# The first expert layer's input and the query weights begin one word into longer rooms

## The chip, the cores and the metric

The kernel runs on one core of a Trainium2 chip. A core has five engines that run side by side, each with its own instruction stream: TensorE (PE, matrix products; its weight loads are shown as PEld), VectorE (DVE), ScalarE (ACT), GpSimd (POOL) and SyncE (SP, which only issues transfers here). They share an on-chip memory of 128 partitions; PE writes its results into a second memory, PSUM, from which ACT and DVE take them. The metric is the device time of one execution in microseconds (us). The kernel before takes 1811.01 us (median of 3 runs, 1810.87 to 1811.89).

## The reference: what is computed

One layer of a decoder, for 512 tokens of width 1024 and 256 memory tokens, all in float32. The hidden state is normalized and projected, three mixers run on it (causal pooling, a sparse attention with 16 heads, a cross-attention into the memory), their outputs are gated, merged and added. The second half is the part that the change touches:

```python
def block(xb):                       # xb: 128 normalized tokens
    q = (xb @ w_q).reshape(n, PEER_HEADS, 2, PEER_HALF)
    s = jnp.einsum('nhpc,hpkc->nhpk', q, sub_keys)
    s_top, i_top = lax.top_k(s, PEER_TOPK)
    ...
    ids = jnp.take_along_axis(cand_i, best_pos, axis=-1)
    gate = jax.nn.softmax(best_s, axis=-1)
    act = jax.nn.gelu(jnp.einsum('nd,nhkd->nhk', xb, u[ids]), approximate=False)
    return jnp.einsum('nhk,nhkd->nd', gate * act, v[ids])
```

It is a layer of 128 x 128 = 16,384 experts of one neuron each. A token picks 16 experts for each of 8 heads by the sums of two sub-key scores; `u` is the experts' first layer, `v` the second. A last normalization gives the output.

## The kernel before

**Products of three parts.** TensorE's fast float32 type (float32r) keeps fewer bits. So each operand is split into a high part (the rounded value, an ACT copy, L133) and a low part (the rest, a subtraction on DVE or POOL, L134), and a product is high x high + high x low + low x high. `mm3_steps` (L154, L161) issues it: for eight contraction steps of 128, three matmuls each, 24 in all, that add up in one PSUM tile. The weights are the stationary side (128 x 128, loaded anew for each matmul); the token side moves, 512 columns for all tokens.

**The feed.** `feed` holds the list of all weight tiles in the order of use. `fetch` issues a tile's load on SP (L78), `part` splits it into `wh` and `wl`, `take` hands it to the matmuls and runs the two ahead by one or two tiles. Most tiles live in one pool with two rooms per part. The list can name another pool for a tile, with three rooms per part: `opool` for three of the four weight pieces of the output projection's second half, and `qpool` for the query weights from the third on (14 of 16).

**The input of the first layer.** `hfh` and `hfl` are the high and low part of the normalized tokens, transposed: 128 partitions, eight contraction steps of 512 words. `transpose_split` writes them, per token block in two halves: a transpose on PE (L192), the high part by ACT (L195), the low part by DVE (L196).

**Who reads them.** `q_mm`, 16 query tiles, all 512 columns. `hidden`, 128 tiles of the first layer, 352 columns, since the first token block and the 32 tokens after it go another way (their experts' rows are gathered one by one). The first tile of either kind takes `mm3_steps`' other order (L154); all others are L161.

**The order of the work from the output projection on.** The output projection (L1166: here the tokens' parts are stationary and the weights move) ends in the normalization and the transposes. Then come the 16 query tiles, each followed by eight matmuls for its scores (L1250) while DVE picks the best (MAX8 and others). Then `lead`: 70 first-layer tiles, whose results wait in HBM, beside the selection on DVE and the gate matrices on PE (one-hot matmuls of 128 columns in float16, L1475, evacuated by ACT at L1478). Last `experts`: 56 first-layer tiles, each beside the second layer of the tile before (18 matmuls of 512 columns, L1634), then 72 second-layer tiles alone. POOL gathers single rows for the first token block all the while. The order on each engine is written out by hand.

**Where things lie.** Pools are stacks from the left and the right end of the memory, tiles follow each other in the order of their allocation, and a tile of four bytes takes 32. Small tiles named `pad` stand in many pools. The `wh`, `wl`, `hfh`, `hfl`, `hnh`, `hnl`, `wgh` and `wgl` tiles all begin at a multiple of 64 bytes, and so does every one of their rows that a matmul reads. `hfh`, `hfl` and behind them the pool `n2` (the tokens, the normalization's rows, and the `opool` rooms) lie on the left; when `n2` is closed, `wv2` with the second layer's weights takes its place, beginning with the tile `seen`. Of `seen` one column is written, to make POOL wait for a load. The query weights' rooms, the sub-keys `skt` and the scores lie in a pool on the right.

Of the kernel before, what the change touches and what calls it, by code (L numbers as in the profile page):

```python
# [10 lines left out]
F32 = mybir.dt.float32  # L11
F32R = mybir.dt.float32r
# [9 lines left out]
T = 512  # L22
NB = 4
D = 1024
KD = 8
# [30 lines left out]
        yield from x  # L56


class Feed:


# [20 lines left out]
    def part(self, n):  # L82
        while self.np < min(n, len(self.specs)):
            key, src, nk, m, eng, other = self.specs[self.np]
            pool, bufs = (self.pool, 2) if other is None else (other[0], 3)
            hi = pool.tile([128, nk, m], F32R, tag=self.tag + "h", name="wh", bufs=bufs)
            lo = pool.tile([128, nk, m], F32R, tag=self.tag + "l", name="wl", bufs=bufs)
            self.split(hi, lo, self.raw.pop(self.np)[0].rearrange("p (k n) -> p k n", n=m), eng or self.nc.gpsimd)
            self.w[self.np] = (hi, lo)
            self.np += 1  # L90
# [20 lines left out]
def layer(ctx: ExitStack, tc: tile.TileContext, A: dict, out: bass.AP, dbg=None):  # L111
# [8 lines left out]
    def sbuf(stack, name, side="left"):  # L120
        return stack.enter_context(tc.tile_pool(name=name, bufs=1, side=side, reuse_waits="tile"))

    def psum(tag, shape, bufs=2, dt=F32):
        return ps.tile(shape, dt, tag=tag, name=tag, bufs=bufs)
# [469 lines left out]
    for c in cross_order:  # L594
        n = int(c[1]) if c[1:].isdigit() else None
# [442 lines left out]
    for at in attention():  # L1038
# [5 lines left out]
        while done < goal:  # L1044
            c = next(filler, None)
# [55 lines left out]
    hrow = dram.tile([X, D], F32, name="hrow")  # L1101
    idd = dram.tile([X, 128], I32, name="idd")
    hp_ = sbuf(ctx, "hp")
    hfh = hp_.tile([128, KD, T], F32R, name="hfh")
    hfl = hp_.tile([128, KD, T], F32R, name="hfl")
    n2s = ExitStack()
    n2 = sbuf(n2s, "n2")
    opool.append(n2)
# [47 lines left out]
    for half, tags in ((0, "SSoo"), (1, "zzSS")):  # L1156
# [12 lines left out]
        if half == 0:  # L1169

            for k2 in range(4):
                w = feed.take(("o", 0, k2))
# [120 lines left out]
    for hp in range(16):  # L1293
        if hp < 15:
            p = psum("z", [128, T])
# [273 lines left out]
    def vfetch(m, eng=nc.sync):  # L1569
        if m < 128:  # L1570
            j = order[m]
            VR[m] = wv2.tile([128, 1024], F32, tag="wr", name="wr", bufs=5)
            eng.dma_start(VR[m], A["v_rows"][j * 128:(j + 1) * 128])
# [155 lines left out]
    gath = seq(*[gathered(b) for b in range(GB)])  # L1729
    ost2.close()  # L1730
    wv2 = sbuf(hst, "wv2")
    seen = wv2.tile([128, 224], F32, name="seen")
    vfetch(0)
    vfetch(1)
    gload(0)
# [109 lines left out]
```

## Time and profile before

| what | value |
| --- | --- |
| median of 3 runs | 1811.01 us |
| the profiled execution: its own time | 1810.61 us |
| the profiled execution: span from first to last instruction | 1808.8 us |
| mean granted TensorE clock | 0.999 |
| PE busy, matmuls | 1787.7 us, 10098 |
| DVE, ACT, POOL busy | 1360.5, 837.7, 770.6 us |

The span is the time between the first and the last instruction that the profiler recorded; the execution's own time has the start and the end around it. Busy times are unions of an engine's instructions; matmuls overlap in the array, so their durations are longer than their distances. A group's row has the line, the engine and operation, the tile written and the tiles read, the shape, the count, the busy time and the mean duration in ns, and then the idle time before it. The chain is followed back from the last instruction, at each step to what released it.

### The profile page before, as it was taken

The numbers are of one execution on the slowest core, as the hardware profiler recorded it, in microseconds if no ns is written. First come the engines' busy times: TensorE is split into PE (matmuls) and PEld (weight loads), VectorE is DVE, ScalarE is ACT, GpSimd is POOL, SyncE is SP. The second block draws the span as 40 slices with busy tenths as digits, with TensorE's granted clock in tenths as the row PEclk, the third lists the DMA queues.
The fourth block names the chain that finished last, engine by engine and source line by source line (L and its number), as shares of the span: only waits on it lengthen the run. The fifth ranks groups of instructions, "written<-read, shape, count | busy, mean of one in ns | idle before, by whom it ended". The sixth has DMA issues, their size and how long they took to land.

```text
span 1808.8 us, 27962 instructions
## 1 busy us (share of the span) xinstructions
PE 1787.7 (99%) x10098; PEld 1586.5 (88%) x10098; DVE 1360.5 (75%) x2814; ACT 837.7 (46%) x1476; POOL 770.6 (43%) x595
## 2 busy tenths in 40 slices
PE   8999999999999999999999999999999999999998
PEld 7988888888888888999999998999999998888886
DVE  5453147766544369999898859998898999888886
ACT  6434257777642333464555543333334333333334
POOL 3333555555643333511222026666656664333320
PEclk9999999999999999999999999999999999999999
DMA  6225632112223432376999899999999999999992
GB/s 225 90 84 168 223 108 59 48 59 71 65 76 111 168 132 91 114 240 215 344 356 326 297 380 410 409 375 392 373 361 368 377 369 376 384 382 382 378 372 105
DMA packets 157147, 445.94 MB, mean 247 GB/s; under 512 B 15969, under 2 KB 61697, under 8 KB 154322
## 3 DMA queue, kind: packets, MB, share of 16 engines
q1 hardware_dynamic: 88050, 262.78, 40.4%
q0 software_dynamic: 41840, 152.10, 22.3%
q10 hardware_dynamic: 27120, 29.30, 4.9%
q8 instruction: 79, 1.29, 0.3%
q14 instruction: 58, 0.48, 0.1%
HBM read 402.11 MB, written 47.24 MB: 248 GB/s over the span
## 4 chain that ended last, share of the span: by engine, by line
PE 92%; DVE 3%; ACT 3%; POOL 1%; issue 1%; DMA 0%; DVEq 0%; SPq 0%; ACTq 0%; POOLq 0%
PE z L161 49%; PE S L1634 10%; PE tr L1634 10%; PE o L1634 9%; PE S L905 1%; PE tr L937 1%; PE S L1166 1%; PE o L953 1%; PE o L424 1%; ACT pr L918 1%; PE o L1475 1%; PE tr L1475 1%; PE S L1475 1%; PE o L1250 1%; DVE pr L915 1%
## 5 line engine op out<-in xcount | busy, mean ns | idle before, releaser
L133 ACT ACTIVATE wh<-wr 128x1024 fp32r<-128x1024 f32 (+2 forms) x365 | 372.3, 1025 | 164.4 <-PE z L161 45.1
L134 POOL TENSOR_TENSOR wl<-wr,wh 128x1024 fp32r<-128x1024 f32 (+2 forms) x110 | 242.8, 2208 | 318.0 <-ACT wh L133 269.7
L161 PE MATMUL z<-hfh,wh 128*128 128x352 f32 (+1 forms) x1136 | 375.5, 332 | 0.0
L161 PE MATMUL z<-hfl,wh 128*128 128x352 f32 (+1 forms) x1136 | 373.4, 330 | 0.0
L134 DVE TENSOR_TENSOR wl<-wr,wh 128x1024 fp32r<-128x1024 f32 x255 | 305.8, 1216 | 80.7 <-ACT wh L133 79.8
L1498 POOL DMA_INDIRECT ug<-in_v_rows_dram,ids x128 | 176.1, 1375 | 199.3 <-DVE x1g L1518 179.9
L1498 POOL DMA_INDIRECT ug<-in_u_rows_dram,ids x128 | 193.7, 1514 | 104.6 <-DVE ug L1512 85.2
L161 PEld LDWEIGHTS z<-hfl,wh 128*128 128x128 f32 x1136 | 214.1, 188 | 6.3
L161 PEld LDWEIGHTS z<-hfh,wh 128*128 128x128 f32 x1136 | 213.5, 188 | 6.9 <-ACT wh L133 0.5
L161 PE MATMUL z<-hfh,wl 128*128 128x352 f32 (+1 forms) x1136 | 213.3, 330 | 0.1
L161 PEld LDWEIGHTS z<-hfh,wl 128*128 128x128 f32 x1136 | 189.2, 188 | 5.1 <-POOL wl L134 0.4
L1215 ACT ACTIVATE hg<-z 128x352 f32<-128x352 f32 x128 | 59.5, 465 | 279.2 <-PE z L161 277.3
L133 ACT ACTIVATE wgh<-gh 128x384 fp32r<-128x384 f32 x128 | 67.4, 526 | 232.1 <-DVE gh L1613 230.3
L1518 DVE SCALAR_TENSOR_TENSOR x1g<-ug,wgt,x1g 128x1024 f32<-128x1024 f32 x128 | 163.9, 1280 | 1.1
L1512 DVE SCALAR_TENSOR_TENSOR ug<-ug,hf 128x1024 f32<-128x1024 f32 x128 | 152.3, 1217 | 5.9 <-DMA ug<-in_u_rows_dram,ids 5.9
L161 PE MATMUL z<-hnh,wh 128*128 128x512 f32 x384 | 150.7, 393 | 0.0
L161 PE MATMUL z<-hnl,wh 128*128 128x512 f32 x384 | 150.3, 391 | 0.0
L1401 POOL DMA_INDIRECT ux<-in_u_rows_dram,idx x32 | 52.1, 1629 | 171.8 <-DVE ux L1409 169.1
L926 POOL TENSOR_SCALAR pr<-pr,sm,gsig 128x128 f32<-128x128 f32 (+3 forms) x128 | 78.1, 613 | 77.9 <-DVE sm L1000 49.0
L134 DVE TENSOR_TENSOR wgl<-gh,wgh 128x384 fp32r<-128x384 f32 x128 | 71.8, 561 | 37.2 <-ACT wgh L133 37.2
L941 DVE TENSOR_TENSOR PB<-tr,PB 128x128 fp32r<-128x128 f32 (+3 forms) x128 | 62.5, 488 | 49.2 <-ACT PB L940 48.5
L161 PE MATMUL z<-hnh,wl 128*128 128x512 f32 x384 | 99.2, 393 | 0.0
(410 smaller groups left out, 3590.3 us busy)
## 6 DMA issues: line engine op xcount, KB each, us to landing
wr<-in_u_t_dram SPq DMA_DIRECT2D x128, 512.0 KB, 6.6
wr<-in_v_rows_dram SPq DMA_DIRECT2D x128, 512.0 KB, 9.0
wr<-in_w_z_dram SPq DMA_DIRECT2D x48, 512.0 KB, 3.6
gd<-stg ACTq DMA_DIRECT2D x11, 2048.0 KB, 15.4
hg<-hd SPq DMA_DIRECT2D x72, 176.0 KB, 9.2
gj<-gd SPq DMA_DIRECT2D x8, 1408.0 KB, 11.9
go<-gd SPq DMA_DIRECT2D x8, 1408.0 KB, 12.9
hd<-hg SPq DMA_DIRECT2D x60, 176.0 KB, 5.6
```

The costliest lines, as they stand in the source:

```text
L133: s.activation(hi, src, AF.Copy)
L134: (eng or v).tensor_tensor(lo, src, f(hi), op=OP.subtract)
L161: pe.matmul(p, w[a][:, k], xs(x[b], k), start=k == 0 and a == 0 and b == 0, stop=k == nk - 1 and a == 1)
L926: g.tensor_scalar(pr[:, 0:n], pr[:, 0:n], sm, gsig[:, qb, c:c + 1], op0=OP.mult, op1=OP.mult)
L941: return lambda: v.tensor_tensor(lo, pt[:, 0:qb + 1], f(hi), op=OP.subtract)
L1215: s.activation(hg[:, X:], p[:, X:NT], AF.Gelu)
L1401: g.indirect_dma_start(out=XR[k], out_offset=None, in_=A["u_rows"], in_offset=bass.IndirectOffsetOnAxis(ap=idx[:, k:k + 1], axis=0))
L1475: pe.matmul(pg[:, n], oa[:, t_ // 2, :, t_ % 2], ob[:, r, t_ // 2, :, t_ % 2], start=n == 0 and r == 0, stop=n == 3 and r == 1, skip_group ...
L1498: g.indirect_dma_start(out=row, out_offset=None, in_=src, in_offset=bass.IndirectOffsetOnAxis(ap=ids[:, b, k:k + 1], axis=0))
L1512: v.scalar_tensor_tensor(row, row, 1.0, hf[:, b], op0=OP.mult, op1=OP.mult, accum_out=act[:, m:m + 1])
L1518: v.scalar_tensor_tensor(X1[b], rows.pop(m), wgt[:, m - 128:m - 127], X1[b], op0=OP.mult, op1=OP.add)
L1634: pe.matmul(acc_o[2 * b + half], a[:, b * 128:(b + 1) * 128], c[:, half], start=k == 0 and i == 0, stop=k == 127 and i == 2)
```

## The change

A helper `behind` makes a tile that is 64 words longer than the data, and returns the view that begins at word AT = 1 of it. `hfh` and `hfl` are made by it, and so are the `wh` and `wl` rooms of the feed's tiles that live in another pool (`opool` and `qpool`). Everything that writes or reads them uses the shifted view. `seen` becomes 128 words (512 bytes) shorter, as much as the rooms of `hfh` and `hfl` become longer together, so that the tiles behind it keep their places.

```diff
+AT = 1
+
+
+def behind(pool, name, k, n, **kw):
+
+    t = pool.tile([128, k * n + 64], F32R, name=name, **kw)
+    return t[:, AT:AT + k * n].rearrange("p (k n) -> p k n", n=n)
+
 class Feed:
...
             pool, bufs = (self.pool, 2) if other is None else (other[0], 3)
-            hi = pool.tile([128, nk, m], F32R, tag=self.tag + "h", name="wh", bufs=bufs)
-            lo = pool.tile([128, nk, m], F32R, tag=self.tag + "l", name="wl", bufs=bufs)
+            if other is None:
+                hi, lo = (pool.tile([128, nk, m], F32R, tag=self.tag + c, name="w" + c, bufs=bufs) for c in "hl")
+            else:
+                hi, lo = (behind(pool, f"w{c}", nk, m, tag=self.tag + c, bufs=bufs) for c in "hl")
...
-    hfh = hp_.tile([128, KD, T], F32R, name="hfh")
-    hfl = hp_.tile([128, KD, T], F32R, name="hfl")
+    hfh, hfl = behind(hp_, "hfh", KD, T), behind(hp_, "hfl", KD, T)
...
-    seen = wv2.tile([128, 224], F32, name="seen")
+    seen = wv2.tile([128, 96], F32, name="seen")
```

## The prediction

> **What bounds the kernel now.** I read the page first, then the groups of instructions by shape, the chain of waits in order of time, and the busy times by stage. The page says which engine fills the span and what the chain consists of.
>
> ```profile
> PE 1787.7 (99%) x10098; PEld 1586.5 (88%) x10098; DVE 1360.5 (75%) x2814; ACT 837.7 (46%) x1476; POOL 770.6 (43%) x595
> ...
> PE 92%; DVE 3%; ACT 3%; POOL 1%; issue 1%; DMA 0%; DVEq 0%; SPq 0%; ACTq 0%; POOLq 0%
> PE z L161 49%; PE S L1634 10%; PE tr L1634 10%; PE o L1634 9%; PE S L905 1%; PE tr L937 1%; PE S L1166 1%; PE o L953 1%; PE o L424 1%; ACT pr L918 1%; PE o L1475 1%; PE tr L1475 1%; PE S L1475 1%; PE o L1250 1%; DVE pr L915 1%
> ```
>
> TensorE is busy 99% of the span and 92% of the chain; nearly half of the chain is L161, the line that reads the tiles of this change. The next fence has the busy times by stage: the queries (645 to 745 us), the lead of the first layer with the gates (to 1070), the first layer beside the second (to 1500).
>
> ```profile
> 645.20:745.30 100.10, 100.10 (x515) 85.78 (x514) 91.18 (x647) 32.51 (x48) 39.20 (x18) 1.00 0.29 96
> 745.30:1070.00 324.70, 324.56 (x2518) 321.67 (x2518) 287.29 (x418) 176.35 (x262) 67.74 (x43) 1.00 0.85 292
> 1070.00:1500.00 430.00, 430.00 (x2272) 391.53 (x2271) 384.37 (x521) 159.91 (x217) 280.30 (x183) 1.00 0.99 383
> ```
>
> The columns are length, then PE, PEld, DVE, ACT and POOL busy, granted clock, DMA share and GB/s. PE fills all three stages at a clock of 1.00. So a nanosecond more or less per matmul is paid at once, and an equal one on another engine is not.
>
> **How many matmuls are touched, and what one costs.** The groups by shape count them.
>
> ```profile
> L161 PE MATMUL z<-hfh,wh 128*128 128x352 f32 x1016 | 327.5, 324 | 0.0
> L161 PE MATMUL z<-hfl,wh 128*128 128x352 f32 x1016 | 326.6, 323 | 0.0
> L161 PE MATMUL z<-hfh,wl 128*128 128x352 f32 x1016 | 183.6, 323 | 0.1
> L161 PE MATMUL z<-hfh,wh 128*128 128x512 f32 x120 | 48.0, 400 | 0.0
> L161 PE MATMUL z<-hfl,wh 128*128 128x512 f32 x120 | 46.8, 390 | 0.0
> L161 PE MATMUL z<-hfh,wl 128*128 128x512 f32 x120 | 29.7, 389 | 0.0
> ```
>
> L161 streams the two tiles 3 x 1016 = 3048 times with 352 columns and 3 x 120 = 360 times with 512; the first tile of either kind (L154, 24 each, below) makes it 3072 and 384. These durations overlap, so what counts is the distance from one start to the next, which the chain of waits gives as the length of a run over its count.
>
> ```profile
> 35.01 5.74 PE o L354 x48
> ...
> 634.14 4.11 PE z L154 x24
> ...
> 639.38 5.84 PE S L154 x24
> ...
> 651.68 5.46 PE z L161 x24
> 657.13 0.89 PE o L1250 x8
> ...
> 877.52 15.41 PE z L161 x96
> ```
>
> A 512-column matmul takes 5.46 / 24 = 227.5 ns of the path, a 352-column one 15.41 / 96 = 160.5 ns. The difference over 160 columns gives 0.419 ns a column; 352 columns are then 147.5 ns and 512 are 214.5 ns, and either has about 13.0 ns beside its columns. I use these four numbers throughout.
>
> The second half of the output projection (L1166) has weights in the same longer rooms, as the moving side, for three of its four weight pieces: each piece feeds two contraction steps with three products for four token blocks, so 3 x 2 x 3 x 4 = 72 more with 512 columns. Touched in all: 3072 + 384 + 72 = **3528 matmuls**; 3072 of 352 columns and 456 of 512.
>
> **The change part by part.**
>
> *No instruction is added, removed or reordered*; the operands' addresses alone move. The sum therefore has one term that matters, 3528 times the change x of one matmul's distance, and small ones on other engines.
>
> *The moving side, 4 bytes past a multiple of 64.* The trace has no full-rate matmul with such a start. The nearest rows: in the attention scores (L905) the keys KK and the queries Q begin 32 bytes past a multiple of 64, because the one-column tile `has`, which takes 32 bytes, lies ahead of them in its stack; pool maps (poolh, pooll) beside them begin on a multiple.
>
> ```profile
> 285.69 0.39 PE L905 MATMUL S<-KK,Q 128*128 128x512 f32 x1
> 285.92 0.40 PE L161 MATMUL z<-poolh,wh 128*128 128x512 f32 x1
> 286.15 0.39 PE L161 MATMUL z<-pooll,wh 128*128 128x512 f32 x1
> ...
> 284.48 0.34 PE L905 MATMUL S<-KK,Q 128*128 128x384 f32 x1
> 284.66 0.49 PE L937 MATMUL tr<-ident,pr 128*128 128x128 f32 x3
> ```
>
> The L905 matmul at 285.69 takes 0.23 us to the next start, and the aligned one after it also 0.23. With 384 columns it is 0.18 us, where 384 x 0.419 + 13 = 174 ns are due. A start in the middle of a 64-byte line costs nothing that is seen. A second neighbour is the compression (L569): its rows step by 124 words (496 bytes), so that its 32 starts lie 0, 48, 32 and 16 bytes past such a multiple in turn.
>
> ```profile
> L569 PE MATMUL o<-TP,wc x64: 272/275/275, 135.7 to 154.9; 128*128 128x124 f32 x64
> ```
>
> Shortest, median and longest of its 64 passes are 272, 275 and 275 ns: no residue of 16 stands out, though these plain fp32 passes draw fewer words in a nanosecond. Of odd words there is no row. Bounds for x: above, every pair of words fetched twice, +147.5 ns (below); below, the 13.0 ns beside the columns shrink to what the gate matmuls have, -9.1 ns (below). I take **x = 0**, the reading of both neighbours.
>
> *The stationary side* (14 query weights, 4 bytes in). A weight load runs beside the matmul before it. The 256-column matmuls of L354 above follow each other every 5.74 / 48 = 119.6 ns, each with its own fp32 load, so a load holds the path for no more than that; under the 227.5 ns of a query matmul it is hidden. Bounds: 0, and doubled loads, 239.2 - 227.5 = 11.7 ns on 14 x 24 = 336 matmuls, 3.9 us; taken 0, as the cover is nearly twice the load.
>
> *The other engines that write or read at odd words.*
>
> ```profile
> L195 ACT ACTIVATE hfh<-tr x4: 595/596/597, 620.8 to 639.2; 128x512 fp32r<-128x512 f32 x4
> L196 DVE TENSOR_TENSOR hfl<-tr,hfh x4: 679/686/691, 621.4 to 640.0; 128x512 fp32r<-128x512 f32 x4
> ...
> L133 ACT ACTIVATE wh<-wr x26: 1042/1062/1066, 588.9 to 741.7; 128x1024 fp32r<-128x1024 f32 x26
> L134 POOL TENSOR_TENSOR wl<-wr,wh x23: 2388/2405/2686, 590.0 to 742.8; 128x1024 fp32r<-128x1024 f32 x23
> ```
>
> ACT and DVE write the input in eight pieces each (half are in these rows). One query needs 1.06 us of ACT and then 2.41 of POOL, against a period of 5.46 + 0.89 = 6.35 us: even a doubled POOL split (1.06 + 4.82 = 5.88) stays hidden, and three rooms let it run ahead. At two and a half times (1.06 + 6.03 = 7.09) the cover would be gone and PE would stand 0.7 us per query, 10 us over 14. One POOL split of the output weights is on the chain, with the matmuls behind it:
>
> ```profile
> 610.00 2.40 POOL wl L134
> 612.41 0.04 issue
> 612.45 7.85 PE z L1166 x32
> ```
>
> Doubled, it costs 2.4 us once; the eight ACT writes of 0.60 us, all doubled and all on the path, 4.8. Bounds 0 to +7.2 us; taken 0, the end that the unchanged L569 passes are nearer to.
>
> *Room.* hfh and hfl push the tiles behind them 512 bytes on, `seen` gives the 512 bytes back, and the six weight rooms of either pool move what follows by multiples of 256 bytes. The loads into those tiles keep their sizes and order on SP's queue, no wait is added and no queue is passed: 0.
>
> Sum: 1810.61 us (the profiled execution: span 1808.8 and 1.81 around it) + 3528 x 0 + 0 = 1810.6 us; the median of the runs shown is 1811.01, 0.4 above it, so **1811.0 us**.
>
> **The rivals.**
>
> *One fetch more per matmul (slower).* If PE reads the row in short lines, a start inside a line touches one more, 3528 times, and it decides as soon as the 13.0 ns do not swallow it. A line of 16 bytes is 4 columns, 1.68 ns: 5.9 us, 1817; of 32 bytes 3.35 ns: 11.8 us, 1823; of 64 bytes 6.7 ns: 23.6 us, 1835. The L905 rows speak against the last, L569 weakly against the first. [...] No run here shows such a line yet.
>
> *Pairs (far slower).* At 0.419 ns a column PE draws 2.4 words each nanosecond, the fastest reader in this trace. If it gets them as aligned pairs, and a start on an odd word makes each pair two fetches, the columns double: 3072 x 147.5 + 456 x 214.5 = 453 + 98 = 551 us, 2362; if only every second pair straddles a line, half of it, 275 us, 2086. It decides from the first odd start on, in all three stages. Against it: the gate matmuls (L1475) read 2-byte elements every 4 bytes, every second matmul from an odd element on.
>
> ```profile
> 854.58 0.63 PE L1475 MATMUL tr<-ob,oa 128*128 128x128 f16 x8
> 855.04 0.62 PE L1475 MATMUL S<-ob,oa 128*128 128x128 f16 x8
> ```
>
> Eight of them take 0.46 us, 57.5 ns each; 128 columns are 53.6 ns by the slope above, so the odd starts cannot double anything, though a pair of 2-byte elements is not a pair of words. [...]
>
> *The start leaves a collision (faster).* Weights and input begin on the same 64-byte phase now, and each fp32r matmul has 13.0 ns beside its columns. The gate matmuls above have only 57.5 - 53.6 = 3.9. If the common phase makes the difference, 9.1 x 3528 = 32 us go, 1779; half of it 1795. Against it: L905's half-line start has the same 0.23 us, but there both sides are moved alike, as with the queries here; the first layer's own weights stay where they are.
>
> That the change doesn't do what it says is no rival: the offset is one element of a 4-byte type in the tile itself, and every reader and writer of the tiles goes through the shifted view.
>
> **How the numbers follow.** About 0.2% (3.6 us) is what a measurement here can tell from no change. No change: 0.47, 1808 to 1814. One fetch more: 0.19. Pairs: 0.14. Collision gone: 0.20. Slower is 0.19 + 0.14 = 0.33, faster 0.20, same 0.47. The range goes from 1785 (most of the collision case, 0.05 left out) to 1836 (all of the extra fetch); the pairs (0.14) are left out, so 0.81 lies inside. Its likeliest part is 1808 to 1814.
>
> **What would show it.** In the changed profile a run of 96 in the lead should last 15.4 us and one of 24 in the queries 5.46. An extra fetch shows as 15.6 to 16.1 and 5.50 to 5.62; pairs as durations of some 470 ns instead of 323; a collision gone as 14.5. If the query runs alone change, it is the stationary side; if the first layer's alone, the relation of the two sides. POOL's splits near 2.4 us show that odd words cost it nothing. The prediction is wrong if runs of 96 leave 15.4 by over 0.1 us, or if PE begins to wait for ACT or POOL.

## The result: 0.6% slower

| | before | after |
| --- | --- | --- |
| median of 4 runs | 1810.94 us (1810.38 to 1811.89) | 1822.16 us (1821.93 to 1822.23) |
| span of the profiled execution | 1808.8 us | 1820.5 us |
| mean granted TensorE clock | 0.999 | 0.999 |

The changed kernel takes 1.0061 times as long [1.0048, 1.0073], 11.2 us more. The prediction said no change, 1811.0 us, and took 1808 to 1814 for the likeliest part of a range from 1785 to 1836; the kernel became slower. All lines of the kernel stand about ten further down now: L161 became L172, L154 L165, L1166 L1176, L1634 L1644, L133 and L134 L144 and L145, L195 and L196 L206 and L207.

The page of the changed kernel first: busy times, and the chain's share by engine.

```profile
PE 1799.7 (99%) x10098; PEld 1595.3 (88%) x10098; DVE 1360.4 (75%) x2814; ACT 838.4 (46%) x1476; POOL 767.9 (42%) x595
...
PE 92%; DVE 3%; ACT 2%; POOL 1%; DMA 1%; issue 1%; SPq 0%; DVEq 0%; ACTq 0%; POOLq 0%
```

The counts are the same, and PE is busy 12.0 us longer (1787.7 before). On the chain DMA rounds to 1% now, for loads in the first 30 us; yet where the output projection begins, ahead of the first touched matmul, the two profiles still differ by 0.21 us only (586.89 and 587.10). So the same matmuls stand further apart. Which ones, the chain of waits tells (start, length, what). Rows of the kernel before that the prediction did not need:

```profile
621.17 5.49 PE S L1166 x24
...
645.22 5.57 PE z L161 x24
...
740.53 3.87 PE z L161 x24
...
760.70 2.86 POOL wl L134
...
1069.91 1.38 PE S L1634 x6
...
1085.83 1.71 PE S L1634 x6
...
1106.15 3.86 PE z L161 x24
...
1495.54 3.86 PE z L161 x24
```

And the rows of the changed kernel that answer to these and to the prediction's 651.68 and 877.52:

```profile
608.86 11.52 PE z L1176 x48
...
621.26 5.65 PE S L1176 x24
...
645.82 5.76 PE z L172 x24
652.47 5.71 PE z L172 x24
...
744.96 3.85 PE z L172 x24
749.69 51.03 PE z L172 x312
...
883.61 15.73 PE z L172 x96
...
1079.03 1.36 PE S L1644 x6
...
1107.11 3.92 PE z L172 x24
...
1507.11 3.92 PE z L172 x24
```

The same places, by their starts: the second query at 645.22, now 645.82 (+0.60); the lead's first full tile at 740.53, now 744.96 (+4.43); the end of the lead at 1069.91, now 1079.03 (+9.12); the last first-layer tile at 1495.54, now 1507.11 (+11.57); the span +11.7. So the queries from the second on cost 3.83 us, the lead 4.69, the first layer beside the second 2.45, what lies ahead of the second query 0.60, and the end 0.1. For one matmul:

| matmul | before | after | more |
| --- | --- | --- | --- |
| query, 512 columns | 5.46 / 24 = 227.5 ns | 5.71 / 24 = 237.9 ns | 10.4 ns |
| output projection, weights moving, 512 columns | 5.49 / 24 = 228.8 ns | 5.65 / 24 = 235.4 ns | 6.7 ns; 8.9 for the touched |
| first layer in the lead, 352 columns | 15.41 / 96 = 160.5 ns | 15.73 / 96 = 163.9 ns | 3.3 ns |
| first layer beside the second, 352 columns | 3.86 / 24 = 160.8 ns | 3.92 / 24 = 163.3 ns | 2.5 ns |

In a run of 24 of the output projection only 18 are touched (three of four weight pieces), so its 0.16 us are 8.9 ns for each of those. By these prices the touched matmuls cost some 13 us (an estimate). Delays that are gone took a part back: the waits for a POOL split at 610.00 and at 760.70 (the run of 312 at 749.69 now passes that place unbroken), and 0.35 us in the L1634 run of 1.71 us at 1085.83, whose neighbours take 1.36.

The groups by shape agree: 327 ns instead of 324 for the first layer's passes, 410 instead of 400 for the queries'.

```profile
L172 PE MATMUL z<-hfh,wh 128*128 128x352 f32 x1016 | 332.0, 327 | 0.0
...
L172 PE MATMUL z<-hfh,wh 128*128 128x512 f32 x120 | 49.1, 410 | 0.0
```

The engines that write the shifted tiles (shortest, median and longest instruction in ns, 586 to 755 us):

```profile
L145 POOL TENSOR_TENSOR wl<-wr,wh x24: 1997/2003/2407, 590.2 to 751.4; 128x1024 fp32r<-128x1024 f32 x24
```

POOL's split of a shifted piece takes 2.00 us where it took 2.40. So the start one word in made POOL's split faster and PE's matmuls slower.

### The profile page after: what moved, and what is told of

It is laid out like the page before. It is cut to its first block, busy times and chain, and to the rows that moved or that the text cites. A ratio compares the mean times of both kernels' runs of the same rounds, so it can differ in the third digit from the quotient of the medians.

```text
span 1820.5 us, 27962 instructions
## 1 busy us (share of the span) xinstructions
PE 1799.7 (99%) x10098; PEld 1595.3 (88%) x10098; DVE 1360.4 (75%) x2814; ACT 838.4 (46%) x1476; POOL 767.9 (42%) x595
## 4 chain that ended last, share of the span: by engine, by line
PE 92%; DVE 3%; ACT 2%; POOL 1%; DMA 1%; issue 1%; SPq 0%; DVEq 0%; ACTq 0%; POOLq 0%
PE z L172 49%; PE S L1644 10%; PE tr L1644 10%; PE o L1644 9%; PE S L916 1%; PE tr L948 1%; PE S L1176 1%; PE o L964 1%; PE o L435 1%; ACT pr L929 1%; PE o L1485 1%; PE S L1485 1%; PE tr L1485 1%; PE o L1260 1%; DVE pr L926 1%
## 5 line engine op out<-in xcount | busy, mean ns | idle before, releaser
L144 ACT ACTIVATE wh<-wr 128x1024 fp32r<-128x1024 f32 (+2 forms) x365 | 373.1, 1026 | 167.4 <-PE z L172 45.3
L172 PE MATMUL z<-hfh,wh 128*128 128x352 f32 (+1 forms) x1136 | 381.2, 336 | 0.0
L172 PE MATMUL z<-hfl,wh 128*128 128x352 f32 (+1 forms) x1136 | 378.3, 333 | 0.0
L145 POOL TENSOR_TENSOR wl<-wr,wh 128x1024 fp32r<-128x1024 f32 (+2 forms) x110 | 234.8, 2135 | 330.1 <-ACT wh L144 282.1
L145 DVE TENSOR_TENSOR wl<-wr,wh 128x1024 fp32r<-128x1024 f32 x255 | 306.2, 1218 | 87.9 <-ACT wh L144 74.1
L172 PEld LDWEIGHTS z<-hfh,wh 128*128 128x128 f32 x1136 | 213.3, 188 | 7.8 <-ACT wh L144 0.5
L172 PEld LDWEIGHTS z<-hfl,wh 128*128 128x128 f32 x1136 | 213.4, 188 | 7.2
L172 PE MATMUL z<-hfh,wl 128*128 128x352 f32 (+1 forms) x1136 | 217.5, 333 | 0.0
L172 PEld LDWEIGHTS z<-hfh,wl 128*128 128x128 f32 x1136 | 191.7, 188 | 5.8
L144 ACT ACTIVATE wgh<-gh 128x384 fp32r<-128x384 f32 x128 | 67.3, 526 | 219.2 <-DVE gh L1623 215.6
L172 PE MATMUL z<-hnh,wh 128*128 128x512 f32 x384 | 150.8, 393 | 0.0
L172 PE MATMUL z<-hnl,wh 128*128 128x512 f32 x384 | 150.3, 391 | 0.0
L172 PE MATMUL z<-hnh,wl 128*128 128x512 f32 x384 | 99.2, 393 | 0.0
L145 DVE TENSOR_TENSOR wgl<-gh,wgh 128x384 fp32r<-128x384 f32 x128 | 71.2, 556 | 37.2 <-ACT wgh L144 37.2
```

The lines of the kernel that those rows point to most:

```text
L144: s.activation(hi, src, AF.Copy)
L145: (eng or v).tensor_tensor(lo, src, f(hi), op=OP.subtract)
L172: pe.matmul(p, w[a][:, k], xs(x[b], k), start=k == 0 and a == 0 and b == 0, stop=k == nk - 1 and a == 1)
```

## The experiments

The open questions: is it the start or the longer rooms; the moving side or the stationary one; and which starts cost. The theories: **one fetch more** (a start off a line's boundary touches one line more), **pairs** (an odd word splits each pair), **the relation of the two sides**, and, after the first runs, **the last line** (a row that ends one word into a line) and **the steps** (a matmul's distance takes only certain values). A distance is a run's length on the chain over its count.

### Other starts in the same rooms

Six kernels differ from the changed one in one number, in words of 4 bytes: 0, 2, 4, 8, 15 and 16.

```diff
-AT = 1
+AT = 0
```

> The longer rooms alone: every operand begins at the start of its room again (word 0), all else as in the changed kernel. If the start inside the line costs the 11.2 us, this is back at the kernel before, 1811 us within 2 us, with runs of 96 in the lead at 15.41 us and query runs of 24 at 5.46. If the rooms' place (512 bytes further, weights' rooms 256 bytes longer) costs it, it stays near 1822, with 15.73 and 5.71.

1811.06 us, ratio 0.9999 [0.9989, 1.0008]. Its chain has the runs of the kernel before:

```profile
651.82 5.46 PE z L172 x24
...
877.75 15.41 PE z L172 x96
```

The room and the places behind it cost nothing; all 11.2 us come from the start.

> Start 8 bytes in, an even word. If only odd words cost (pairs of 8 bytes), 1811 us: 160.5 ns per 352-column matmul in the lead, 227.5 per query matmul. If lines of 16 or 32 bytes are read, it costs what 4 bytes cost: 1822 us, 163.9 and 238 ns.

At 8 bytes one execution took 1813.74 us, against a median of 1811.10 for the kernel before.

```profile
651.85 5.57 PE z L172 x24
...
878.91 15.43 PE z L172 x96
```

The first layer pays 0.2 ns per matmul, the queries 4.6 (5.57 / 24 = 232.1).

> Start 16 bytes in. Pairs of 8 bytes or lines of 16: 1811 us, 160.5 and 227.5 ns. Lines of 32 bytes or more: about 1822 us, 163.9 and 238 ns.

At 16 bytes: 1811.34 us, one execution; 15.42 in the lead, and in the queries:

```profile
652.51 5.60 PE z L172 x24
```

The queries pay 5.8 ns, which is 2 us over all of them, and the total hardly shows it. A part comes back beside the second layer, where a run of 24 takes 3.84 us (160.0 ns) and not the 3.86 (160.8) of the kernel before: about 1 us over 56 tiles (an estimate). The starts of 32, 60 and 64 bytes have the same 3.84 there.

> Start 32 bytes in. The keys of the attention have that start and cost nothing there: 1811 us, 160 ns for 352 columns, 227 for 512. If every start off a multiple of 64 costs the wide matmuls one more line of 64 bytes, as 8 and 16 bytes in did (232 to 233 ns), the 384 query matmuls cost 6 ns, 2.3 us: 1813.

At 32 bytes: 1812.69 us, one execution, beside a median of 1811.69 for the kernel before on that chip.

```profile
652.80 5.46 PE z L172 x24
...
878.65 15.41 PE z L172 x96
```

A start in the middle of 64 bytes is as fast as an aligned one, which the prediction read off L905.

> Start 64 bytes in: all starts are multiples of 128 bytes now, where before they were odd multiples of 64. If no line is longer than 64 bytes, 1811 us, 160.5 and 227.5 ns. If lines of 128 bytes are read, the kernel before already touches one too many (12 for 352 columns, 17 for 512), and this one is faster: 147 to 150 ns and 214 to 217 ns, up to 13 ns x 3528 = 46 us less, 1765 us.

At 64 bytes: 1810.80 us, ratio 0.9997 [0.9988, 1.0007], with 5.46 to 5.48 in the queries, 15.41 to 15.42 in the lead, and beside the second layer:

```profile
1107.14 3.84 PE z L172 x24
```

So it makes no difference to the time whether the rows begin at odd or even multiples of 64 bytes.

> Start 60 bytes in, an odd word, the last of its line. If every odd word costs (pairs of 8 bytes), 1822 us as at 4 bytes. If only the first words of a line cost, as the probe's cells say (230.6 ns at 512 columns, 160.0 at 352), 1811 to 1813 us: lead runs of 96 at 15.4 us, query runs of 24 at 5.46 to 5.55.

At 60 bytes, an odd word: 1811.45 us (1810.95 for the kernel before beside it, one execution each).

```profile
651.50 5.51 PE z L172 x24
...
877.87 15.41 PE z L172 x96
```

The first layer pays nothing at an odd word, the queries 2.1 ns. With that the pairs fall, and so does one fetch more: at 8, 16 and 60 bytes the rows of the first layer would touch just as many lines of 64 bytes as at 4, and at 8 and 60 as many lines of 32 or 16, and yet cost 0.2 ns or less where 4 bytes cost 3.3. The theory also has one price for a fetch at 512 and at 352 columns, where 10.4 and 3.3 ns were measured.

### Which side

The helper takes the start as an argument; in one kernel the weights' rooms get 0, in the other the input's.

```diff
-def behind(pool, name, k, n, **kw):
+def behind(pool, name, k, n, at=AT, **kw):
...
-                hi, lo = (behind(pool, f"w{c}", nk, m, tag=self.tag + c, bufs=bufs) for c in "hl")
+                hi, lo = (behind(pool, f"w{c}", nk, m, 0, tag=self.tag + c, bufs=bufs) for c in "hl")
```

> Only hfh and hfl begin one word in; the weights' rooms stay longer but begin at word 0. Theory: the moving side pays. Then about 0.7 us of the output projection (72 matmuls at some 10 ns) goes and the rest stays: 1821.5 us, lead runs of 96 at 15.73 us, query runs of 24 at 5.71 to 5.76. Rival, the stationary side of the queries pays their part: query runs back to 5.46 and 3.8 us less, 1818.

1822.07 us, ratio 1.0058 [1.0041, 1.0074].

```profile
622.07 5.49 PE S L1176 x24
...
652.94 5.66 PE z L172 x24
...
883.56 15.73 PE z L172 x96
```

```diff
-    hfh, hfl = behind(hp_, "hfh", KD, T), behind(hp_, "hfl", KD, T)
+    hfh, hfl = behind(hp_, "hfh", KD, T, 0), behind(hp_, "hfl", KD, T, 0)
```

> Only the weights in the longer rooms begin one word in, hfh and hfl at word 0. Theory (moving side pays): the output projection's 72 matmuls cost 0.7 us, 1811.8 us, query runs of 24 at 5.46. Rival (stationary side pays): query runs at 5.71, 16 x 0.25 = 4 us, 1815 us.

1812.89 us against 1811.69, ratio 1.0007 [0.9998, 1.0017].

```profile
621.66 5.66 PE S L1176 x24
...
652.50 5.58 PE z L172 x24
...
879.67 15.41 PE z L172 x96
```

The moving side pays nearly all. The lead is slow (15.73) when the input is shifted alone and as before (15.41) when the weights are; its weights are aligned in both, and the queries, whose two sides are moved alike, are slow too. So unequal starts, as in the lead, and equal ones, as in the queries, are both slow. The output projection, where the weights move, is slow (5.66) only with the weights shifted. In the queries the moving side takes 227.5 to 235.8 ns (5.66 / 24), the stationary side alone to 232.5 (5.58 / 24), both together to 237.9. So in this kernel the stationary start costs the queries 5 ns by itself and 2 beside the other; the expectation had 0 or 10.

The split of the shifted weights on POOL, in the input's kernel and then in the weights' kernel:

```profile
L145 POOL TENSOR_TENSOR wl<-wr,wh x24: 2377/2395/2439, 590.7 to 751.1; 128x1024 fp32r<-128x1024 f32 x24
```

```profile
L145 POOL TENSOR_TENSOR wl<-wr,wh x25: 1999/2005/2407, 590.5 to 753.7; 128x1024 fp32r<-128x1024 f32 x25
```

It goes with the start of its own tiles.

### The disputed cost by itself

The kernel before, with chains of 24 equal matmuls put in behind the transposes of the normalized tokens, ahead of the pooling mixer. They read the tokens' high part as the moving side and the low part as the stationary one, and their results go nowhere. `n` is the width, `off` the moving side's start and `so` the stationary one's, in words past a multiple of 64 bytes; `at` is where a chain's word 0 lies.

```diff
+    hnf, lnf = (x.rearrange("p k n -> p (k n)") for x in hn)
+    for n, at, off, so in [(512, 32, 0, 0), (512, 32, 1, 0), ...]:
+        p = psum("z", [128, T])
+        for i in range(24):
+            w0, m0 = 512 * (i % 7) + 128 * (i % 4) + so, 512 * (i % 7) + at + off
+            pe.matmul(p[:, 0:n], lnf[:, w0:w0 + 128], hnf[:, m0:m0 + n], start=i == 0, stop=i == 23)
```

> The kernel before with 106 x 24 matmuls more, right after the normalized tokens are there, whose results nobody reads: widths 128 to 512, moving starts 0 to 32 words past a multiple of 64 bytes, stationary starts 0 to 8 words past; each matmul with its own weight load. It measures the cost by itself, with no other engine at work, some 400 us more in all. Theory (an odd word splits every pair of 8 bytes): all odd starts cost alike, 238 to 240 ns at 512 columns and 163 to 164 at 352, at 3, 5, 7, 9, 15, 17 and 31 words as at 1; even ones at most 233 and 160. Rival (only the place inside a line counts, an extra line read): the cost grows or falls with the offset and is the same for 1 and 2 words. Stationary starts: no cost at 512 columns under the theory; under the rival of a slower load it shows at 256 columns first.

Its timeline, one row for each chain (start, length, count); here with 512 columns at words 1, 9, 15 and 32, then with 352 at word 1 and word 15:

```profile
33.56 5.92 PE L386 MATMUL z<-hnh,hnl 128*128 128x512 f32 x24
78.51 5.85 PE L386 MATMUL z<-hnh,hnl 128*128 128x512 f32 x24
100.95 5.69 PE L386 MATMUL z<-hnh,hnl 128*128 128x512 f32 x24
140.16 5.61 PE L386 MATMUL z<-hnh,hnl 128*128 128x512 f32 x24
149.47 4.10 PE L386 MATMUL z<-hnh,hnl 128*128 128x352 f32 x24
195.82 4.00 PE L386 MATMUL z<-hnh,hnl 128*128 128x352 f32 x24
```

A row's length holds 23 distances and the last matmul's own duration (0.40 or 0.39 us at 512 columns, 0.32 at 352). So the distances are 240, 237, 230 and 227 ns, then 164 and 160. The distances by start, in ns, from the settled part of the chains:

| columns | word 0 | 1 | 2 | 3 | 5 | 7 | 9 | 15 | 16 | 17 | 31 | 32 |
| --- | --- | --- | --- | --- | --- | --- | --- | --- | --- | --- | --- | --- |
| 512 | 233 | 240.0 | 237.3 | 231.4 | 233.5 | 230.5 | 236.9 | 230.6 | 233.2 | 240.0 | 229.5 | 226.7 |
| 352 | 161.2 | 163.8 | 160.0 | 160.0 | 161.7 | 159.9 | 163.4 | 160.0 | 159.9 | 166.1 | 160.0 | 158.3 |

Odd words are not alike: of them 1, 9 and 17 are the dearest at both widths; 3, 7, 15 and 31 lie among the aligned ones. Nor are even words free: word 2 costs as much as word 9 at 512 columns. Words 0, 16 and 32 are all aligned, and 512 columns take 233 in two of these chains and 226.7 in the third. And the cost of word 1 over word 0 is no smooth function of the width: 0.0 ns at 128 columns, 4.1 at 256, 1.5 at 288, 1.6 at 320, 2.6 at 352, 2.4 at 384, 6.5 at 416, 8.7 at 448, 6.8 at 480.

The probe also moved the stationary side, with 512 columns. Here it begins at word 1, first with the moving side at word 0, then with both at word 1:

```profile
437.11 5.65 PE L386 MATMUL z<-hnh,hnl 128*128 128x512 f32 x24
442.59 5.85 PE L386 MATMUL z<-hnh,hnl 128*128 128x512 f32 x24
```

Settled, these are 226.9 and 236.5 ns, where the stationary side at word 0 has 233.1 and 240.0. So here a stationary start at word 1 saves 6 and 3.5 ns, and in the queries it cost 5 and 2. At words 2 and 8 it changes nothing (233.3, 233.2), at word 4 it saves as much as at word 1 (226.6); with 352 and 256 columns and the moving side at word 0, word 1 changes next to nothing (0.1 to 0.3 ns). At 512 columns the two sides' places count together, then, and no fixed price belongs to the stationary side. The moving side's word 1 costs in every pair measured at this width: with the stationary side at word 0, 8.3 ns in the queries and 6.9 here.

### Where a row begins and where it ends

A row of 352 columns from word 1 ends one word into a line of 16 words, one from word 15 does not. Two kernels tell begin and end apart. The first layer streams 354 columns, from two words earlier, into PSUM columns that are not used. With a start of 1 its rows begin at word 15 and end one word into a line; with a start of 3 they begin at word 1 and end three words in.

```diff
-        mm3(p[:, X:NT], w, (hfh, hfl), KD, xs=lambda x, k: x[:, k, t0 + X:T], **order)
+        mm3(p[:, X - 2:NT], w, (hfh, hfl), KD, xs=lambda x, k: x[:, k, t0 + X - 2:T], **order)
```

> The changed kernel, but the first layer streams 354 columns, two tokens more ahead whose results nobody reads. A row then begins at the last word of a line and still ends one word into a line. Two columns more are 2 x 0.419 ns x 3072 = 2.6 us. Head theory (a begin at word 1 costs): the first layer's 8 us go, 1817 us, lead pitch 161 ns. Tail theory (a single word in the last line costs): 1825 us, 164.5 ns.

1813.55 us, one execution.

```profile
653.07 5.71 PE z L172 x24
...
882.17 15.42 PE z L172 x96
```

> The same 354 columns with the start 12 bytes in: a row begins at word 1 of a line and ends three words into one. The queries begin at word 3, some 4 ns over aligned each, 1.5 us. Head theory: the first layer pays as in the changed kernel, 1823 us, lead pitch 164.5 ns. Tail theory: 1815 us, 161 ns.

1812.27 us, one execution.

```profile
651.98 5.50 PE z L172 x24
...
878.29 15.42 PE z L172 x96
```

Neither costs the first layer anything: 15.42 / 96 = 160.6 ns, for two columns more. The end at word 1 is not the cause, and the begin at word 1 alone is not either. (The queries keep their 512 columns: 5.71 at word 1, 5.50 at word 3.)

> A second probe at the same place, 31 shapes four times over in mixed order, 24 matmuls each, begin and end of the row set apart. Head theory: begin at word 1 costs whatever the end is (510, 498 and 504 columns from word 1 as 512 from word 1, some 12 ns over the aligned row of the same width; 350, 354, 344 from word 1 some 3 to 4), and 498 and 354 columns from word 15, 510 and 350 from word 3 (all of which end one word into a line) cost nothing beside their columns. Tail theory: the other way round. If both are needed, only 512, 496 and 352 columns from word 1 cost.

This is the probe with 31 pairs of width and start, four chains of 24 for each, in mixed order. Distances in ns, means of the four:

| columns | word 0 | 1 | 3 | 9 | 15 |
| --- | --- | --- | --- | --- | --- |
| 344 | | 157.8 | | 159.9 | |
| 350 | 160.0 | 160.0 | 159.8 | | |
| 352 | 160.7 | 163.4 | 160.0 | | 160.0 |
| 354 | 160.0 | 160.0 | | | 160.6 |
| 496 | 226.7 | 229.6 | | | 220.0 |
| 498 | 226.6 | 231.1 | | | 221.3 |
| 504 | | 233.2 | | 227.4 | |
| 510 | | 233.4 | 231.7 | | 226.7 |
| 512 | 233.5 | 240.0 | 231.4 | | 230.4 |

The four chains of most pairs agree within 0.3 ns; the others jump between two values (510 columns from word 3: 226.6 once, 233.3 three times). Neither theory of one end holds: 350 columns from word 3 end at word 1 and are free, and 354 from word 1 are free. What stands out are values that come back at several widths: 160.0, 220.0, 226.7, 233.3 and 240.0, all multiples of 6.67 ns, which is 16 columns at the prediction's 0.419 ns.

### Width alone, and the steps

If the steps alone decided, the kernel before with 354 columns (from word 14) might be as fast as with 352, or faster:

> The kernel before with 354 columns in the first layer (two tokens more ahead, whose results nobody reads; 8 bytes before a multiple of 64). If the width alone holds the distance at 160.0 ns, also beside the second layer, where it is 161.0 now, 56 x 24 x 1.0 = 1.4 us go and two columns cost nothing: 1809.5 us. If columns are paid as they come, 0.84 ns x 3072 = 2.6 us more: 1813.6.

1815.58 us, ratio 1.0023 [1.0014, 1.0032], with the queries unchanged at 5.46 and the lead at

```profile
878.88 15.58 PE z L161 x96
```

15.58 / 96 = 162.3 ns where word 0 has 160.5 and where 354 columns from words 15 and 1 have 160.6. So the start counts beside the width, and an even one (14) can cost.

> A third probe at the same place, 136 shapes in mixed order, 32 matmuls each. Step theory (starts are spaced in multiples of 16 columns, 6.67 ns): the distance is flat at 160.0 over a stretch of widths around 352 and at 220, 226.7 or 233.3 around 500, and a begin at word 1 only moves the edges of the stretches; the cost then appears where a width lies at an edge, at 352 and 512 among others. Column theory: the distance rises by 0.83 ns with every second column, for all begins alike, and word 1 costs a constant on top.

The probe with widths of 336 to 368 and 480 to 512 in steps of two, at words 0, 1, 3 and 15, chains of 32. Its timeline has for 352 columns at words 0 and 1, 354 at words 1 and 3, and 480 at words 0 and 1:

```profile
514.41 5.28 PE L386 MATMUL z<-hnh,hnl 128*128 128x352 f32 x32
...
170.39 5.39 PE L386 MATMUL z<-hnh,hnl 128*128 128x352 f32 x32
...
578.59 5.29 PE L386 MATMUL z<-hnh,hnl 128*128 128x354 f32 x32
...
796.91 5.49 PE L386 MATMUL z<-hnh,hnl 128*128 128x354 f32 x32
...
780.03 7.13 PE L386 MATMUL z<-hnh,hnl 128*128 128x480 f32 x32
...
416.36 7.42 PE L386 MATMUL z<-hnh,hnl 128*128 128x480 f32 x32
```

By 31 distances and the last duration (0.32 to 0.33 us, at 480 columns 0.38 to 0.39) that is 160, 163.5, 160 and 166.5 ns, then 218 and 227. Each start is at its lowest at one width and dearer than another start at the next. Over the settled part of all chains, in ns:

| columns | word 0 | 1 | 3 | 15 |
| --- | --- | --- | --- | --- |
| 336 | 153.3 | 156.6 | 153.4 | 153.3 |
| 352 | 160.0 | 163.4 | 160.1 | 160.0 |
| 354 | 160.0 | 160.0 | 166.7 | 160.0 |
| 356 | 160.0 | 166.6 | 160.0 | 160.0 |
| 368 | 166.7 | 170.0 | 166.7 | 166.7 |
| 480 | 217.8 | 226.7 | 213.3 | 213.3 |
| 496 | 226.6 | 226.7 | 220.0 | 220.0 |
| 512 | 232.6 | 240.0 | 231.4 | 230.5 |
| mean over the 17 widths to 368, less columns / 2.4 | 14.2 | 16.0 | 13.4 | 12.6 |
| mean over the 17 widths from 480, less columns / 2.4 | 18.5 | 22.7 | 15.9 | 16.3 |

The distance does not grow evenly by the column: 74 of the 136 chains lie within 0.3 ns of a multiple of 6.67 ns (153.3, 160.0, 166.7; 213.3, 220.0, 226.7, 233.3, 240.0), the others between (163.4, 217.8, 231.4). It does not even always rise: at word 0, 338 columns take 160.0 and 340 take 154.9. So the step theory holds in part, and single widths mislead. Its other half, that word 1 only moves the edges of the steps, does not hold. The two last rows take the steps out: on average word 1 is the worst of the four, by 1.8 ns over word 0 near 352 and by 4.1 near 512 (it is the dearest by over 0.5 ns at 22 of the 34 widths), and words 3 and 15 are better than word 0. No kernel tried beats the one before: the two medians that lie lowest, at starts of 0 and of 16 words, have intervals around 1.

## Why the prediction was wrong, point by point

**What bounds the kernel: right.** PE fills the stages (in the changed kernel it is busy for all 107.20 us from 645.80 to 753, all 327.00 to 1080 and all 432.00 to 1512) and pays each nanosecond of distance at once; 3528 touched matmuls and 11.2 us make 3.2 ns each, and the stages' sums (0.60 + 3.83 + 4.69 + 2.45) come from the touched matmuls' rows.

**x = 0, "the reading of both neighbours": this step failed.** x is 10.4 ns for a query, 8.9 in the output projection, 3.3 in the lead and 2.5 beside the second layer. The neighbours lay at other kinds of start: L905 at 32 bytes, which is free (5.46 and 15.41 at 32 bytes in the chain above), and L569 at 0, 16, 32 and 48 bytes with another kind of product. The prediction itself says "Of odd words there is no row". It then took the value of rows that could not carry it.

**"13.0 ns beside its columns": a wrong picture.** The slope of 0.419 ns and the 13.0 ns came from two widths. The slope is right over a step (6.67 ns for 16 columns), but the distance rests at 160.0 from 350 to 356 columns at word 0, and what is left beside the columns averages 14.2 ns near 352 and 18.5 near 512. So no fixed 13.0 ns could swallow an extra fetch, or be won. The rival of a collision was built on that slack and fell: of the seven starts tried in the kernel none gains more than the 0.8 ns beside the second layer (160.0 for 160.8), which 16, 32, 60 and 64 bytes have.

**One fetch more: the size by accident, the mechanism not.** Its 32-byte case gave 1823, and 1822 was measured. But it prices 352 and 512 columns alike (3.35 ns), and the runs show 3.3 and 10.4; at 8, 16 and 60 bytes it should cost the first layer as much as at 4, or nearly, and the chain shows 15.43, 15.42 and 15.41, against 15.73.

**Pairs: wrong, as given.** An odd word at 60 bytes is free for the first layer and costs a query 2.1 ns. Nothing near the doubled columns of that theory (214.5 ns more for 512 of them) shows in any chain: at 512 columns the dearest start has 240.0 ns where the cheapest has 226.7, 6%, and only some odd words lie that high.

**The stationary side, 0 with a bound of 11.7 ns: nearly.** Shifted alone it costs a query 5 ns, inside the bound; all of that kernel's difference is 1.2 us with an interval that holds 1. But the cover that the prediction argued with does not explain it: in the probe the same shift made the 512-column chain 6 ns faster.

**The other engines, 0 with a bound of +7.2 us: right in what it costs.** None of PE's waits for ACT, DVE and POOL grew by over 0.1 us (two for ACT's `hfh`, 0.2 us each before, are 0.3 now). POOL was not bounded below: its split became 0.40 us shorter, and the two that stood on the chain at 610.00 and 760.70 left it (the runs of 48 at 608.86 and of 312 at 749.69 pass there).

**Room and places: right**, 1811.06 at a start of 0.

**What would show it.** "If the query runs alone change, it is the stationary side" was half wrong: the queries have more to lose on the moving side (8.3 ns) than on the other (5), and the lead changed too.

**What stays open.** That the moving side's start makes nearly all of the 11.2 us is shown, by the starts in the kernel and by the shift of one side alone. That the distance often rests on multiples of 6.67 ns, and that width and start decide together, is shown by the chains. Why word 1 is worst (9 and 17 were dear too), why the aligned 512-column rows rest at 227 in some chains and at 233 in others, and why the stationary side's shift costs in the kernel and saves in the probe, was not found.

## What to carry to other kernels

Rows of neighbouring alignments did not price a start that none of them had (0 was read off them, 2.5 to 10.4 ns were measured); where PE sets the time with thousands of such matmuls, 3 ns each were 0.6%, so the pair of width and start is worth a measured chain of a few dozen matmuls, and then a run of the kernel itself: the probe had 233 ns for aligned rows whose queries run at 227.5. Keep float32r moving rows from beginning one word past a multiple of 64 bytes: of the four starts of the third probe it was the dearest on average (16.0 ns beside the columns near 352 where word 0 has 14.2, and 22.7 near 512 where word 0 has 18.5). In the queries words 2 and 4 cost 4.6 and 5.8 ns, while starts at 32 and 64 bytes were free (runs of 5.46 and of 5.46 to 5.48 us, where the kernel before has 5.46). Two widths give the mean slope, and not what one width pays: at word 0 the distance stays at 160.0 ns from 350 to 356 columns and is 166.7 at 368.

## What the runs showed of the hardware that was not expected

- The distance between float32r matmuls, each with its own weight load, often rests at multiples of 6.67 ns (160.0, 166.7; 213.3, 220.0, 226.7, 233.3, 240.0; 74 of 136 chains), and two columns more can cost nothing, cost 6.7 ns (356 for 354 columns at word 1) or save 5 (340 for 338 at word 0).
- The same 512-column chain from an aligned row runs at 227 ns in one place and at 233 in another.
- The stationary side's start counts at 512 columns, and not in one direction: one word in costs a query 5 ns (227.5 to 232.5) and saves 6 in the probe (233.1 to 226.9).
- POOL's split of 128 x 1024 words takes 2.00 us where its result and one source begin at word 1 or 2 of their rooms, and 2.40 at words 0, 3, 4, 8, 15 and 16 (medians of 2002 to 2005 ns, and of 2395 to 2412).
